# The first modulation of a two-layer trunk in 512 features, summed on TensorE, and its later parts in 1 MB tiles

## The chip, the cores and the metric

One core of a Trainium2 chip runs the whole program. The metric is the device time of one execution in microseconds (us), the median of several runs. The engines are TensorE (PE, with its weight loads as PEld), VectorE (DVE), ScalarE (ACT), GpSimd (POOL) and SyncE (SP), which here does nothing but issue DMA transfers, in order.

## The reference

Two layers work on 256 tokens of 2048 features. A conditioning vector c gives each layer six modulation vectors, and each mixer and each MLP sees a normed input that these scale and shift:

```python
cond = jax.nn.silu(c)
for i in range(DEPTH):
    mod = (cond @ w_mod[i] + b_mod[i])[:, None, :]
    sh_m, sc_m, g_m, sh_f, sc_f, g_f = jnp.split(mod, 6, axis=-1)
    h = rmsnorm(x, norm_mix[i]) * (1.0 + sc_m) + sh_m
    y = gla_mixer(h, ...) if i % 2 == 0 else fox_mixer(h, ...)
    x = x + (1.0 + g_m) * y
    h = rmsnorm(x, norm_ffn[i]) * (1.0 + sc_f) + sh_f
    x = x + (1.0 + g_f) * conv_ffn(h, ...)
return rmsnorm(x, norm_final)
```

Layer 0 is the gated linear attention (GLA). Its first product is `h @ w_in` with 6160 columns: q and k of 1024 each, v and r of 2048 each, and a of 16. Everything is fp32. `w_mod` has 2048 x 12288 numbers per layer, so that one section of it (sc_m, say) is 16.8 MB.

## The kernel before, in words

**The stream.** Nearly all the work is products of the 256 tokens with weights that are read once. A weight tile is 128 rows (one K tile) by 1024 columns, 512 KB. ACT casts it to a high part `wh`, DVE subtracts for a low part `wl` (`split_w`, L112), and TensorE multiplies wh by the high and low part of h and wl by the high part. In `stream_a` (L603) that is 24 matmuls of 256 columns for a K tile, in `stream_b` (L637, for v) 12 of 512. `next_w` (L561) hands out the tiles in the order of the list `plan`; DVE and ACT split up to AHEAD = 3 tiles ahead of TensorE, and SP loads ahead as far as the pool `ring` has free buffers. After each K tile `tick` may run a piece of side work.

**The staging of GLA's input.** h of K tile k needs sc_m and sh_m of 128 features, which are sums over all 2048 rows of `w_mod`. BLOCKS = (8, 8) splits the K tiles in two blocks. Before the stream starts, `drain_startup` makes sc_m and sh_m for the first 8 K tiles (1024 features) out of sixteen 1 MB tiles `wm`: for the first four K rows 8 matvecs each on TensorE (L265, "direct"), for the other twelve one accumulating DVE instruction over 1024 columns each (L271), then 8 transposes (L304), two DVE reductions (L308) and small adds. In between stand the load of x, its transposes (`load_x`, L441), the copies and squares on ACT (L443, L462), the sum over features (L483) and the reciprocal root (`token_rstd`, L492 to L496). Then the pieces q, a, k, v0, v1, r0, r1 run over K tiles 0 to 7 and their sums are put aside in SBUF by `fold` (L707). Meanwhile the tasks for sc_m and sh_m of the features 1024 to 2047 run in the background, in 512 KB tiles of the pool `ring`, on DVE. `drain_bg` ends them, and the same pieces run over K tiles 8 to 15.

**What sets the order.** Each engine runs its instructions in order. The order is that in which the program's scheduler placed them, by a simulated timeline of its own; so instructions that stand later in the code can be placed among earlier ones. A load waits on SP for its buffer to come free and for the load eight places ahead, and every load behind it waits too.

**Pools.** `ring` has 7 buffers of 4 KB per partition (weights, narrow wm tiles), `big` 12 of 8 KB (x, wide wm tiles, h, the put-aside pieces).

Of the kernel before, what the change touches and what calls it, by code (L numbers as in the profile page):

```python
# [18 lines left out]
P = 128  # L19
D = 2048  # L20
# [11 lines left out]
RING = 7  # L32
AHEAD = 3
DIRECT = 4
XAFTER = 1
# [5 lines left out]
PEND = 2  # L41
BLOCKS = (8, 8)
FIRST = (6, 0)
# [27 lines left out]
def kernel(  # L71
# [13 lines left out]
    accp = ctx.enter_context(tc.tile_pool(name="accp", bufs=2))  # L85
    tmp = ctx.enter_context(tc.tile_pool(name="tmp", bufs=2))
# [25 lines left out]
    def split_w(src, moving, after=None):  # L112
        n_ = src.shape[-1]
        o1, o2 = (0, 0) if moving else HELD
        hi = tmp.tile([P, WCOLS], F32R, tag="wh", bufs=AHEAD + 1, name=nm("wh"))[:, o1:o1 + n_]
        lo = tmp.tile([P, WCOLS], F32R, tag="wl", bufs=AHEAD + 1, name=nm("wl"))[:, o2:o2 + n_]
        nc.scalar.copy(out=hi, in_=src)  # L117
        with ExitStack() as es:
            if after is not None:
                es.enter_context(tc.issue_after(after))  # L120
            order["v"] = nc.vector.tensor_tensor(out=lo, in0=src, in1=hi.bitcast(F32), op=ALU.subtract).ins  # L121
# [114 lines left out]
    def mod_tasks(l, key, f0=0, fn=D, wide=False, direct=0, defer=False, turn=False):  # L236
# [8 lines left out]
        def chunk(c0, kt, st):  # L245
            def load():
                st[kt] = bigt([P, per, width], "wm") if wide else ringt([P, per, width], "wm")
                src = w_mod[l, kt * P:(kt + per) * P, s * D + c0:s * D + c0 + width]
                with after_startup(not wide):
                    dma = nc.sync.dma_start(out=st[kt], in_=src.rearrange("(k p) m -> p k m", p=P))  # L250
                if wide:
                    startup["loads"].append(dma.ins)

            def f():
                wt = st.pop(kt)
                m0, mn = c0 // P, width // P
                last = kt + per == KT
                if direct and kt == 0:
                    st["p"] = psA.tile([P, 512], F32, tag="a", name=nm("pd"))
                for j in range(per):  # L260
                    k = kt + j
                    col = cT[:, k:k + 1]
                    if k < direct:
                        for m in range(mn):
                            nc.tensor.matmul(st["p"][:, m:m + 1], wt[:, j, m * P:(m + 1) * P], col,  # L265
                                             start=(k == 0 and m == 0), stop=(k == direct - 1), skip_group_check=True)
                    elif k == direct:
                        st["a"] = accp.tile([P, 1024], F32, tag="acc", name=nm("acc"))[:, :width]
                        nc.vector.tensor_scalar(out=st["a"], in0=wt[:, j, :], scalar1=col, scalar2=None, op0=ALU.mult)
                    else:  # L270
                        nc.vector.scalar_tensor_tensor(out=st["a"], in0=wt[:, j, :], scalar=col, in1=st["a"],  # L271
                                                       op0=ALU.mult, op1=ALU.add)
                if last and defer:
                    deferred.append(finish)
                elif last and wide:
                    finish()
# [11 lines left out]
            def finish():  # L288
# [7 lines left out]
                elif turn or wide:  # L296
                    red = tmp.tile([P, 8], F32, tag="red", name=nm("red"))
                else:
                    pt = misc()
                    nc.tensor.matmul(pt[:, :4 * mn], quad, st["r"][:, :4 * mn], start=True, stop=True)  # L300
                for q0 in range(0, mn if turn or wide else 0, 4):
                    pt = psA.tile([P, 512], F32, tag="a", name=nm("pt")) if wide else misc()
# [13 lines left out]
                if defer or turn or wide:  # L316
# [6 lines left out]
                if direct:  # L323
                    nc.vector.tensor_tensor(out=dst, in0=dst, in1=st["p"][:, :mn], op=ALU.add)
# [107 lines left out]
    def load_x():  # L432
        xs = []
        for tt in range(TT):
            xs.append(bigt([P, D], "xtok"))
            nc.sync.dma_start(out=xs[tt], in_=x[0, tt * P:(tt + 1) * P, :])
        for m in range(0, KT, 2):
# [123 lines left out]
    def next_w(kt, cols, hold=None):  # L561
# [3 lines left out]
        run, look = AHEAD if hold is None else hold, RING - 1  # L565
# [5 lines left out]
    def split_to(end, look=RING - 1):  # L571
# [124 lines left out]
    def gla(l, h):  # L696
# [514 lines left out]
    k0 = 0  # L1211
    for nb in BLOCKS:
        for i, c0 in enumerate((0, 1024, 2048, 3072, 4096, 5120)):
            if i == (0 if k0 + nb == KT else 1):
                plan.append((gla_w_in[0], k0, nb, ((6144, RANK),), False))
            plan_stream(gla_w_in[0], range(k0, k0 + nb), [(c0, 1024)], c0 in (2048, 3072))
        k0 += nb
# [11 lines left out]
    def queue_norm(f0, nb, *kind):  # L1229
        queue(mod_tasks(0, "sc_m", f0 * P, nb * P, *kind, turn=True))  # L1230
        queue(mod_tasks(0, "sh_m", f0 * P, nb * P, *kind, turn=True))

    def drain_startup():
        while bg or pending:
            prefetch(WIDE)
            bg_step()

    queue_norm(0, BLOCKS[0], True, DIRECT)
    for _ in range(XAFTER):
        prefetch(WIDE)  # L1240
        bg_step()
    load_x()
    first_h = make_h(0, "m")
    drain_startup()
    bounds = [sum(BLOCKS[:i]) for i in range(len(BLOCKS))]
# [9 lines left out]
    args = gla(0, h)  # L1255
# [79 lines left out]
```

## Time and profile before

| what | value |
|---|---|
| time, median of 3 runs | 2452.31 us (2449.97 to 2458.36) |
| profiled execution: time, span | 2452.57 us, 2450.8 us |
| PE, PEld busy | 2401.6 us, 2313.5 us |
| DVE, ACT busy | 1926.7 us, 1254.9 us |
| moved by DMA | 638.32 MB, mean 260 GB/s |
| first matmul of the stream | 60.90 us after the span's start |
| end of the 8 tiles of block one of every piece, first matmul of K tile 8 | about 206.2 us |

The profiled execution's time is 1.8 us longer than its span, and its time stands 0.26 us from the median. All times within the program are counted from the span's start. "Granted clock" is the share of TensorE's full clock that the profile shows for a stretch of time.

### The profile page before, as it was taken

How to read it: one execution, taken by the hardware profiler on the slowest of the kernel's cores; microseconds unless marked ns; L12 is line 12 of the kernel's file. 1: busy time of each engine (PE TensorE's matmuls, PEld its weight loads, DVE VectorE, ACT ScalarE, POOL GpSimd, SP SyncE). 2: the span in 40 equal slices, each digit the busy share in tenths (PEclk: the TensorE clock that was granted, in tenths of full speed). 3: DMA queues.
4: the chain of work that ended last, by engine and by line, in shares of the span. 5: the costliest groups of instructions: out<-in, count | busy, mean ns of one | idle time of the engine just before them, and what ended most of it. 6: DMA issues, size and time to landing. Idle time of an engine off the chain costs nothing.

```text
span 2450.8 us, 46953 instructions
## 1 busy us (share of the span) xinstructions
PE 2401.6 (98%) x19147; PEld 2313.5 (94%) x19150; DVE 1926.7 (79%) x2587; ACT 1254.9 (51%) x1700; POOL 16.5 (1%) x35
## 2 busy tenths in 40 slices
PE   6999999999999999999999999999999999999998
PEld 6998899899999999999988888999999999999998
DVE  7777989887789999987587898887876777777544
ACT  2456555444655555543454545554655555555433
POOL 0000000000000000000000000000000000000000
PEclk7999999899999999999999999999999999999999
DMA  9897878798668888999589887687677777756553
GB/s 371 281 314 239 301 260 313 277 315 313 201 192 273 304 290 307 308 336 320 182 287 311 302 291 235 222 292 250 220 236 233 233 235 237 230 194 220 192 190 112
DMA packets 184309, 638.32 MB, mean 260 GB/s; under 512 B 23961, under 2 KB 24971, under 8 KB 183708
## 3 DMA queue, kind: packets, MB, share of 16 engines
q1 hardware_dynamic: 183128, 634.12, 76.8%
q8 instruction: 150, 2.46, 0.4%
q10 hardware_dynamic: 964, 1.20, 0.1%
q14 instruction: 67, 0.55, 0.1%
HBM read 633.14 MB, written 2.10 MB: 259 GB/s over the span
## 4 chain that ended last, share of the span: by engine, by line
PE 88%; DVE 5%; DMA 5%; issue 1%; ACT 0%; SPq 0%; DVEq 0%; ACTq 0%
PE pa L614 23%; PE pa L613 23%; PE pa L612 23%; PE pa L650 5%; PE pa L649 5%; PE pa L648 5%; DMA wm<-in_w_mod_dram 4%; DVE wl L121 2%; DVE acc L271 1%; PE pm L483 0%; PE pt L293 0%; PE pm L852 0%; DMA w<-in_gla_w_in_dram 0%; PE pm L1063 0%; PE pm L874 0%
## 5 line engine op out<-in xcount | busy, mean ns | idle before, releaser
L117 ACT CAST wh<-w 128x1024 fp32r<-128x1024 f32 x819 | 855.9, 1048 | 985.4 <-PE pa L613 686.2
L121 DVE TENSOR_TENSOR wl<-w,wh 128x1024 fp32r<-128x1024 f32 x819 | 993.4, 1219 | 315.5 <-ACT wh L117 311.3
L613 PE MATMUL pa<-h,wh 128*128 128x256 f32 x3584 | 992.3, 278 | 2.3 <-DVE h L530 2.3
L614 PE MATMUL pa<-h,wl 128*128 128x256 f32 x3584 | 990.8, 278 | 3.5 <-DVE wl L121 3.5
L612 PE MATMUL pa<-h,wh 128*128 128x256 f32 x3584 | 990.6, 278 | 3.3 <-ACT h L528 1.8
L614 PEld LDWEIGHTS pa<-h,wl 128*128 128x128 f32 x3584 | 673.1, 188 | 7.1 <-DVE wl L121 4.5
L613 PEld LDWEIGHTS pa<-h,wh 128*128 128x128 f32 x3584 | 675.5, 189 | 3.3 <-DVE h L530 3.1
L612 PEld LDWEIGHTS pa<-h,wh 128*128 128x128 f32 x3584 | 673.6, 189 | 4.4 <-ACT h L528 2.2
L271 DVE SCALAR_TENSOR_TENSOR acc<-wm,cT,acc 128x1024 f32<-128x1024 f32 x352 | 451.9, 1284 | 131.0 <-DMA wm<-in_w_mod_dram 129.4
L613 PE MATMUL pa<-op,wh 128*128 128x256 f32 x1920 | 527.9, 277 | 0.4 <-DVE op L546 0.4
L612 PE MATMUL pa<-op,wh 128*128 128x256 f32 x1920 | 527.2, 277 | 0.0
L614 PE MATMUL pa<-op,wl 128*128 128x256 f32 x1920 | 523.6, 277 | 0.4 <-DVE wl L121 0.4
L613 PEld LDWEIGHTS pa<-op,wh 128*128 128x128 f32 x1920 | 360.5, 188 | 0.6 <-DVE op L546 0.6
L612 PEld LDWEIGHTS pa<-op,wh 128*128 128x128 f32 x1920 | 359.8, 188 | 0.0
L614 PEld LDWEIGHTS pa<-op,wl 128*128 128x128 f32 x1920 | 357.3, 188 | 0.8 <-DVE wl L121 0.6
L649 PE MATMUL pa<-wh,h 128*128 128x512 f32 x512 | 200.1, 392 | 0.0
L648 PE MATMUL pa<-wh,h 128*128 128x512 f32 x512 | 198.7, 392 | 0.0
L650 PE MATMUL pa<-wl,h 128*128 128x512 f32 x512 | 194.3, 393 | 0.0
L1115 ACT ACTIVATE y<-u,cw 128x256 f32<-128x256 f32 x176 | 101.8, 599 | 30.9 <-DVE act L1131 28.6
L648 PEld LDWEIGHTS pa<-wh,h 128*128 128x128 f32 x512 | 96.2, 188 | 19.3 <-issue 0.2
L650 PEld LDWEIGHTS pa<-wl,h 128*128 128x128 f32 x512 | 95.9, 188 | 19.5 <-DVE wl L121 0.3
L649 PEld LDWEIGHTS pa<-wh,h 128*128 128x128 f32 x512 | 96.2, 188 | 19.1
(258 smaller groups left out, 1350.6 us busy)
## 6 DMA issues: line engine op xcount, KB each, us to landing
wm<-in_w_mod_dram SPq DMA_DIRECT2D x352, 512.0 KB, 5.2
w<-in_ffn_w_up_dram SPq DMA_DIRECT2D x320, 512.0 KB, 4.5
w<-in_ffn_w_down_dram SPq DMA_DIRECT2D x176, 512.0 KB, 4.5
w<-in_fox_w_in_dram SPq DMA_DIRECT2D x128, 512.0 KB, 5.0
w<-in_gla_w_in_dram SPq DMA_DIRECT2D x96, 512.0 KB, 5.1
wm<-in_w_mod_dram SPq DMA_DIRECT2D x16, 1024.0 KB, 12.3
w<-in_gla_w_out_dram SPq DMA_DIRECT2D x32, 512.0 KB, 6.0
w<-in_ffn_w_up_dram SPq DMA_DIRECT2D x64, 256.0 KB, 4.1
```

The costliest lines, as they stand in the source:

```text
L117: nc.scalar.copy(out=hi, in_=src)
L121: order["v"] = nc.vector.tensor_tensor(out=lo, in0=src, in1=hi.bitcast(F32), op=ALU.subtract).ins
L271: nc.vector.scalar_tensor_tensor(out=st["a"], in0=wt[:, j, :], scalar=col, in1=st["a"], op0=ALU.mult, op1=ALU.add)
L612: nc.tensor.matmul(o, wh[:, ms], rh, start=(first and m % 2 == 0), stop=False, skip_group_check=True)
L613: nc.tensor.matmul(o, wh[:, ms], rl, start=False, stop=False, skip_group_check=True)
L614: nc.tensor.matmul(o, wl[:, ms], rh, start=False, stop=last, skip_group_check=True)
L648: nc.tensor.matmul(o, lh[:, ts_], wh[:, hs_], start=first, stop=False)
L649: nc.tensor.matmul(o, ll[:, ts_], wh[:, hs_], start=False, stop=False)
L650: nc.tensor.matmul(o, lh[:, ts_], wl[:, hs_], start=False, stop=last)
L1115: nc.scalar.activation(y, u, AF.Identity, scale=cw[:, l * 3 + 2, r:r + 1], bias=cw[:, 6 + l, r:r + 1])
```

## The change

Sections and pools first: `ring` has 8 buffers and the look-ahead of the loads is written out as 6, as it was. Up to three background tiles are loaded ahead (PEND = 3; before 2). The split parts have a pool of their own.

What is computed before the stream starts is sc_m and sh_m of the first 512 features (HEAD = 4 K tiles) out of eight 1 MB tiles of 4 K rows by 512 columns. They are summed on TensorE: `cz` holds silu(c), one column in 32, the rest zero, and for each K row a matmul of 32 result rows by 512 columns is made (`early_sum`); the four K rows of a tile go to the four groups of 32 result partitions of one PSUM bank. ACT copies the bank, and one matvec for each 128 features adds the 128 partitions up and turns the sum (`early_finish`). After three of the four tiles of sh_m five filler matmuls are issued (KEEP). x is loaded after two wm tiles.

The pieces q, k and v0 then run over K tiles 0 to 3. During them sc_m of features 512 to 1023 is summed in the background on DVE (1 MB tiles), and the tiles of sh_m are loaded; at the end `finish_late` sums sh_m on TensorE. Then q, k, v0 run over K tiles 4 to 7 and are added to what was put aside; a, v1, r0, r1 run over K tiles 0 to 7. The features 1024 to 2047 follow in the background in 1 MB tiles of the pool `big` and are ended without `turn`: by DVE transposes and one small matmul with `quad`.

```diff
-RING = 7
+RING = 8
+LOOK = 6
-DIRECT = 4
-XAFTER = 1
-PEND = 2
+PEND = 3
+HEAD = 4
+HEADED = ('q', 'k', 'v0')
+KEEP = 5
...
+    cz = bigt([P, KT, 32], "cz")
+    nc.vector.memset(cz, 0.0)
...
+    nc.vector.tensor_copy(out=cz[:, :, 0:1], in_=cT.rearrange("p (k o) -> p k o", o=1))
...
-        k0 = 0
-        for bi, nb in enumerate(BLOCKS):
-            kts = list(range(k0, k0 + nb))
-            k0 += nb
-            if bi > 0:
-                drain_bg()
-            if bi + 1 < len(BLOCKS):
-                for key, c0 in pieces[1:2] + pieces[:1] + pieces[2:]:
-                    fold(key, piece(key, kts, c0))
+        run(HEADED, ALL[:HEAD])
+        drain_bg()
+        finish_late()
+        run(HEADED, ALL[HEAD:BLOCKS[0]])
+        run([key for key, _ in pieces if key not in HEADED], ALL[:BLOCKS[0]])
+        drain_bg()
+        kts = ALL[BLOCKS[0]:]
...
+    def early_sum(key, f0, j):
+        wt = early.pop((key, f0, j))
+        if j == 0:
+            early[key, f0] = psA.tile([P, 512], F32, tag="a", name=nm("pe"))
+        for g in range(4):
+            mm = nc.tensor.matmul(early[key, f0][32 * g:32 * g + 32, :], cz[:, 4 * j + g, :], wt[:, g, :],
+                                  start=(j == 0), stop=(j == 3), skip_group_check=True)
+        return mm.ins
+
+    def early_finish(key, f0):
+        rows_ = t2("er")
+        nc.scalar.copy(out=rows_, in_=early.pop((key, f0)))
+        pt = misc()
+        for m in range(HEAD):
+            nc.tensor.matmul(pt[:, m:m + 1], rows_[:, m * P:(m + 1) * P], one, start=(m == 0), stop=(m == HEAD - 1),
+                             skip_group_check=True)
+        dst = mod[:, SECT[key], f0:f0 + HEAD]
+        b0 = SECT[key] * KT + f0
+        nc.vector.tensor_tensor(out=dst, in0=pt[:, :HEAD], in1=bm[:, b0:b0 + HEAD], op=ALU.add)
...
+    todo = [(key, 0, j) for key in ("sc_m", "sh_m") for j in range(4)]
+    for args in todo[:2]:
+        startup["loads"].append(early_load(*args))
+    xs = fetch_x()
+    for args in todo[2:WIDE]:
+        startup["loads"].append(early_load(*args))
+    load_x(xs)
     first_h = make_h(0, "m")
-    drain_startup()
+    for i, args in enumerate(todo):
+        if i + WIDE < len(todo):
+            startup["loads"].append(early_load(*todo[i + WIDE]))
+        summed = early_sum(*args)
+        if args[2] == 3:
+            early_finish(*args[:2])
+        elif args[0] == "sh_m":
+            pw = psA.tile([P, 512], F32, tag="a", name=nm("pw"))
+            with tc.issue_after(summed):
+                for _ in range(KEEP):
+                    nc.tensor.matmul(pw, fill[:, :P], fill, start=True, stop=True)
...
     def staged_h(m):
-        i = bounds.index(m) if m in bounds else KT
-        if i + 1 < len(BLOCKS):
-            queue_norm(bounds[i + 1], BLOCKS[i + 1])
-            set_pace(6 * BLOCKS[i] - N0)
+        if m == 0:
+            for j, task in enumerate(mod_tasks(0, "sc_m", HEAD * P, HEAD * P, wide=True)):
+                bg.extend((task, (lambda j=j: early_load("sh_m", HEAD, j), lambda: None)))
+            set_pace(HEAD * len(HEADED) - 3)
+        elif m == HEAD:
+            for key in ("sc_m", "sh_m"):
+                queue(mod_tasks(0, key, BLOCKS[0] * P, BLOCKS[1] * P, wide=True))
+            set_pace(6 * BLOCKS[0] - HEAD * len(HEADED) - N0)
         return first_h(m)
```

How the scheduler places this, at three places. In the order lists below, a row is a line of the kernel, an operation, the tiles written and read, and a size; x4 stands for four alike.

TensorE, the start, before (pd: direct matvecs, pm<-ident,xtok: transposes of x) and then with the change (pe: early sums, pw: fillers):

```order
L173 MATMUL pm_110<-ident,crow_101 128x16
L265 MATMUL pd_147<-cT,wm_139 128x1 x16
L265 MATMUL pd_147<-cT,wm_141 128x1 x16
L177 MATMUL pm_114<-ident,rows_103 128x98
L197 MATMUL pm_131<-ident,brow_129 128x96
L197 MATMUL pm_136<-ident,brow_134 128x96
L441 MATMUL pm_168<-ident,xtok_164 128x128
```

```order
L1246 MATMUL pe_239<-wm_153,cz_123 32x512 x3
L1246 MATMUL pe_239<-wm_155,cz_123 32x512 x4
L203 MATMUL pm_137<-ident,brow_135 128x96
L1246 MATMUL pe_271<-wm_237,cz_123 32x512 x4
L1283 LDWEIGHTS fill
L1283 MATMUL pw_276<-fill 128x512
...
L203 MATMUL pm_142<-ident,brow_140 128x96
L431 MATMUL pm_157<-ident,xtok_149 128x128
L431 MATMUL pm_157<-ident,xtok_150 128x128
```

The first transposes of x stood right after the small transposes; now they stand behind the fifth early sum (wm_237, the first tile of sh_m) and its fillers. The other 28 stand behind the sixth, seventh and eighth sum.

SP, the loads that follow the eight early tiles, with the change (w: weight tiles; of the wm tiles L256 loads sc_m, L1239 sh_m, features 512 to 1023):

```order
L571 DMA w_454<-in_gla_w_in_dram 128x1024
L256 DMA wm_382<-in_w_mod_dram 128x4x512
L1239 DMA wm_384<-in_w_mod_dram 128x4x512
L256 DMA wm_386<-in_w_mod_dram 128x4x512
L1239 DMA wm_446<-in_w_mod_dram 128x4x512
L256 DMA wm_500<-in_w_mod_dram 128x4x512
L571 DMA w_456<-in_gla_w_in_dram 128x1024
...
L571 DMA w_547<-in_gla_w_in_dram 128x1024
L1239 DMA wm_545<-in_w_mod_dram 128x4x512
L256 DMA wm_577<-in_w_mod_dram 128x4x512
L1239 DMA wm_613<-in_w_mod_dram 128x4x512
```

Five of the eight tiles are issued after the eighth weight tile (w_454), the last three after the fourteenth (w_547). Before, nothing of this kind stood here: the stream's first block had its modulation whole.

TensorE and then DVE, the passage from K tile 3 to K tile 4, with the change (pa_661: the last bank of v0; h_775: h of K tiles 4 to 7; wl_794: the low part of q's weight tile for K tile 7; pm_698 and pm_765: the finished sums of sc_m and sh_m):

```order
L640 MATMUL pa_661<-wl_665,h_318 128x512
L1246 MATMUL pe_746<-wm_384,cz_123 32x512 x4
L1246 MATMUL pe_746<-wm_446,cz_123 32x512 x4
L1246 MATMUL pe_746<-wm_545,cz_123 32x512 x4
L1246 MATMUL pe_746<-wm_613,cz_123 32x512 x4
L295 MATMUL pm_698<-red_649,quad 128x16
L1255 MATMUL pm_765<-ones,er_763 128x1 x4
L602 MATMUL pa_771<-h_775,wh_682 128x256
```

```order
L124 TENSOR_TENSOR wl_726<-w_583,wh_725 128x1024
L279 TENSOR_REDUCE red_649<-mt_650 128x16
L124 TENSOR_TENSOR wl_794<-w_615,wh_793 128x1024
L311 TENSOR_TENSOR mod<-pm_698,bm 32x4 x4
L315 SCALAR_TENSOR_TENSOR mod<-mod,vec 128x4
L1259 TENSOR_TENSOR mod<-pm_765,bm 128x4
L519 TENSOR_SCALAR hn_776<-hn_776,mod 128x256
```

The sums of sh_m stand between the last matmul of v0 over K tile 3 and the first of q over K tile 4, and on DVE a weight tile's low part stands ahead of the modulation that K tile 4 waits for. Before, K tile 4 followed K tile 3 with nothing between.

More of the change, by code (lines that the diff above doesn't have):

```diff
@@ L248, in load @@
                 src = w_mod[l, kt * P:(kt + per) * P, s * D + c0:s * D + c0 + width]
[L249 to L252, printed above, removed]
+                with after_startup():
+                    nc.sync.dma_start(out=st[kt], in_=src.rearrange("(k p) m -> p k m", p=P))
             def f():
                 wt = st.pop(kt)
-                m0, mn = c0 // P, width // P
                 last = kt + per == KT
-                if direct and kt == 0:
-                    st["p"] = psA.tile([P, 512], F32, tag="a", name=nm("pd"))
                 for j in range(per):
@@ L262, in f @@
                     col = cT[:, k:k + 1]
[L263 to L267, printed above, removed]
+                    if k == 0:
                         st["a"] = accp.tile([P, 1024], F32, tag="acc", name=nm("acc"))[:, :width]
@@ L295, in finish @@
                     red = pt
-                elif turn or wide:
+                elif turn:
                     red = tmp.tile([P, 8], F32, tag="red", name=nm("red"))
@@ L300, in finish @@
                     nc.tensor.matmul(pt[:, :4 * mn], quad, st["r"][:, :4 * mn], start=True, stop=True)
-                for q0 in range(0, mn if turn or wide else 0, 4):
-                    pt = psA.tile([P, 512], F32, tag="a", name=nm("pt")) if wide else misc()
+                for q0 in range(0, mn if turn else 0, 4):
+                    pt = misc()
                     for m in range(min(4, mn - q0)):
@@ L430, with fetch_x, load_x @@
     xT = const.tile([P, KT, T], F32, name="xT")
-    def load_x():
-        xs = []
+    def fetch_x():
+        xs = [bigt([P, D], "xtok") for _ in range(TT)]
         for tt in range(TT):
-            xs.append(bigt([P, D], "xtok"))
             nc.sync.dma_start(out=xs[tt], in_=x[0, tt * P:(tt + 1) * P, :])
+        return xs
+    def load_x(xs):
         for m in range(0, KT, 2):
@@ L564, in next_w @@
         fetched["use"] += 1
-        run, look = AHEAD if hold is None else hold, RING - 1
+        run, look = AHEAD if hold is None else hold, LOOK
         if i < STAGE:
@@ L569, in next_w, with split_to @@
         return splits.popleft()
-    def split_to(end, look=RING - 1):
+    def split_to(end, look=LOOK):
         while fetched["split"] < end:
@@ L1209, in queue_halves, with plan_piece @@
                 queue(mod_tasks(l, key + kind, f0, 1024, defer=f0 > 0 and DEFER))
[L1211 to L1217, printed above, removed]
+    gla_cols = {"q": 0, "k": 1024, "v0": 2048, "v1": 3072, "r0": 4096, "r1": 5120}
+    def plan_piece(key, kts):
+        if key == "a":
+            plan.append((gla_w_in[0], kts[0], len(kts), ((6144, RANK),), False))
+        else:
+            plan_stream(gla_w_in[0], kts, [(gla_cols[key], 1024)], key[0] == "v")
+    for key in HEADED:
+        plan_piece(key, ALL[:HEAD])
+    for key in HEADED:
+        plan_piece(key, ALL[HEAD:BLOCKS[0]])
+    for key in ("a", *gla_cols):
+        if key not in HEADED:
+            plan_piece(key, ALL[:BLOCKS[0]])
+    for key in ("a", *gla_cols):
+        plan_piece(key, ALL[BLOCKS[0]:])
     for g in range(2):
@@ L1228 @@
     load_bmod()
[L1229 to L1242, printed above, removed]
-    first_h = make_h(0, "m")
-    drain_startup()
-    bounds = [sum(BLOCKS[:i]) for i in range(len(BLOCKS))]
@@ new lines, with finish_late @@
+    bounds = [0, HEAD, BLOCKS[0]]
+    def finish_late():
+        for j in range(4):
+            early_sum("sh_m", HEAD, j)
+        early_finish("sh_m", HEAD)
+    def staged_h(m):
+        if m == 0:
[6 more added lines that the diff above has]
+            set_pace(6 * BLOCKS[0] - HEAD * len(HEADED) - N0)
```

37 lines of the change are left out of this document (22 added, 15 removed).

## The prediction

> **What bounds the kernel now.** I read the page first, then TensorE's waits, then tables by stretch of time.
>
> ```profile
> span 2450.8 us, 46953 instructions
> PE 2401.6 (98%) x19147; PEld 2313.5 (94%) x19150; DVE 1926.7 (79%) x2587; ACT 1254.9 (51%) x1700; POOL 16.5 (1%) x35
> PEclk7999999899999999999999999999999999999999
> ```
>
> TensorE is busy for 98% of the span. So a change of this size can gain only where TensorE waits, runs at a low clock, or does work that isn't the product. The clock's low digits are in the first slice, and a little in slice 8. TensorE's waits, all of the time from 206 us on, the three largest:
>
> ```profile
> PE pm L300 <- DVE red L284: 4.0, 4, 1.8
> PE pm L483 <- DVE ss L476: 3.9, 1, 3.9
> PE pa L614 <- DVE wl L121: 2.6, 4, 0.9
> ```
>
> Some 11 us in 2245, so what follows block one is as good as full. The time to be won lies ahead of 206 us. Stretches (us; busy PE, PEld, DVE, ACT, POOL with counts; granted clock; DMA share, GB/s):
>
> ```profile
> 40.00:60.00 20.00, 13.41 (x60) 12.75 (x60) 17.51 (x21) 2.56 (x3) 0.00 (x0) 0.50 0.95 378
> 60.90:64.30 3.40, 2.17 (x9) 1.88 (x9) 3.37 (x8) 3.40 (x6) 0.00 (x0) 0.50 0.00 0
> 64.30:69.90 5.60, 5.60 (x26) 5.60 (x27) 5.60 (x10) 2.06 (x3) 0.00 (x0) 0.51 0.76 201
> 69.90:101.30 31.40, 31.40 (x278) 31.40 (x277) 23.95 (x33) 14.17 (x17) 0.00 (x0) 1.00 0.90 299
> 195.11:198.18 3.07, 0.28 (x4) 0.08 (x2) 1.34 (x2) 1.04 (x1) 0.00 (x0) 1.00 0.84 332
> 198.18:206.20 8.02, 8.02 (x56) 8.02 (x57) 4.26 (x7) 5.07 (x21) 0.00 (x0) 0.79 0.67 209
> ```
>
> A warm stream makes 278 matmuls in 31.40 us: 0.113 us each, 2.71 us for a K tile of 24. The first 9.0 us (60.9 to 69.9) make only 35 of them, at half clock. Ahead of the stream stand 60.9 us, and at the end of block one 3.07 us of waiting and a dip of the clock. What ends last before the stream:
>
> ```profile
> 49.18 7.88 DVE L271 SCALAR_TENSOR_TENSOR acc<-wm,cT,acc 128x1024 f32<-128x1024 f32 x6
> 57.12 1.97 PE L304 MATMUL pt<-ident,acc 128*128 128x128 f32 x8 [5.67 <-DVE acc L271]
> 60.25 1.09 ACT L528 ACTIVATE h<-hn,mod 128x256 fp32r<-128x256 f32 x2 [4.87 <-DVE mod L324]
> 60.90 1.22 PE L612 MATMUL pa<-h,wh 128*128 128x256 f32 x4 [1.82 <-ACT h L528]
> ```
>
> So the order is: the sixteenth wm tile, DVE's sums, transposes, h.
>
> **The change part by part.**
>
> *The start.* Half the wm bytes and all of DVE's sums go. Bytes moved from 0 to 29.0 us and from 0 to 49.2 us, and three stretches:
>
> ```profile
> DMA packets 2885, 10.68 MB, mean 368 GB/s; under 512 B 266, under 2 KB 572, under 8 KB 2629
> DMA packets 5047, 18.93 MB, mean 385 GB/s; under 512 B 419, under 2 KB 725, under 8 KB 4789
> 5.00:30.00 25.00, 21.55 (x99) 19.55 (x99) 13.30 (x18) 7.69 (x14) 0.00 (x0) 1.00 1.03 410
> 915.00:945.00 30.00, 30.00 (x265) 29.94 (x264) 28.02 (x35) 17.60 (x28) 0.00 (x0) 1.00 0.95 327
> 70.00:180.00 110.00, 110.00 (x779) 102.41 (x778) 80.81 (x82) 54.71 (x78) 0.00 (x0) 1.00 0.92 309
> ```
>
> Eight wm tiles, x and the small rows are 10.7 MB: there at 29 us, instead of 18.9 MB at 49. The new tiles have rows of 2 KB. From 915 to 945 us ffn_w_up is loaded largely in such rows, 327 GB/s at a share of 0.95; 4 KB rows give 309 at 0.92. No loss, so I add none.
>
> Then the early sums. Prices of a 512-column fp32 matmul, and of matmuls in different result partitions:
>
> ```profile
> 223.78 1.98 PE L751 MATMUL pm<-wg,aT 17*128 17x512 f32 x4
> L751 PE MATMUL pm<-wg,aT x8: 587/588/692, 223.8 to 230.5; 17*128 17x512 f32 x8
> 290.49 0.22 PE L852 MATMUL pm<-q,k 128*64 128x64 f32 x1
> 290.49 0.22 PE L852 MATMUL pm<-q,kend 128*64 128x64 f32 x1
> 290.99 0.50 PE L650 MATMUL pa<-wl,h 128*128 128x512 f32 x1
> 198.18 1.09 PE L304 MATMUL pm<-ident,acc 128*128 128x128 f32 x8 [2.79 <-DVE acc L271]
> ```
>
> Four of 512 columns take 1.98 us, with the last one's 0.59 us tail: 0.46 us apart at full clock, and 0.93 at half (the 8 transposes: 1.09 us warm, 1.97 at half clock). Attention scores go to partitions 0 to 63 or 64 to 127, and two of them start within the same 0.01 us. So a tile's four column groups cost between 0.46 us (side by side) and 1.84 (in turn), twice that at half clock. I take side by side, because those two rows are the only ones with groups. The Trainium skill speaks to both ends ("TensorE: Matmul & The Clock Gate", Part 3): it has three column tiles at 2.38 times one, and four row tiles at 3.07 times; my estimate from it is 1.84 / 3.07 = 0.60 us for a tile, which would move the sum by less than 1 us. The switch between full and grouped use costs about 0.1 us in the last L852 row and the L650 row after it (0.16 us between last start and next, of which one such matmul is 0.06); some 14 switches lie in the start, where TensorE waits for tiles anyway. The skill's page "TensorEngine Tiling (Array Packing)", Key Properties, says that a change of tiling mode drains TensorE, without a price; by the row it is 1.4 us, hidden.
>
> So sums keep up with the tiles (one each 1.05 MB / 410 GB/s = 2.6 us), and x's chain ends last. ACT's part of it before:
>
> ```profile
> 22.58 0.58 ACT L443 COPY xT<-pm 128x512 f32<-128x512 f32 x1 [16.23 <-PE pm L441]
> 31.03 1.19 ACT L462 ACTIVATE sq<-xT 128x512 f32<-128x512 f32 x2
> 32.23 1.28 ACT L492 ACT_TABLE_LOAD   x1
> 42.73 0.47 ACT L492 ACTIVATE rb<-pm,epsc 128x256 f32<-128x256 f32 x1 [9.22 <-PE pm L483]
> 47.84 1.42 DVE L527 TENSOR_TENSOR hn<-xT,rb 128x256 f32<-128x256 f32 x4
> ```
>
> The first transposes now stand behind the fifth sum: three tiles ahead of the last, 29 - 7.7 = 21.3 us, plus the sum 0.9, five fillers at half clock 2.2 (a 512-column pass of the warm stream takes 2.71 / 12 = 0.226 us, twice that is 0.45), four transposes 1.0: 25.4. ACT's copies and squares took 9.65 us (22.58 to 32.23). They now also wait between batches for the sixth to eighth sum, for which I add 2: 37. Then two copies of sums (1.2), the table load (1.3), rb (0.5), three DVE steps of 0.42 and two of 0.17 (1.6), four hn (1.4), the last add and h (0.8), hand-overs of some 0.03 to 0.1 each (1): 44.8, say 45 us. That is **-15.9 us**, between -19 (no waits in ACT) and +1 (the first rival). The first 9.0 us of the stream are as cold as they were, since TensorE has little to do from 33 to 45 us: 0.
>
> *K tile 3 to 4.* New, and on the path: TensorE has nothing else, as the order shows. Sixteen sum matmuls: 4 x 0.46 = 1.9 us (7.4 in turn). Then ACT's copy 0.58, four matvecs about 0.7 with their tail, the add 0.2, h 0.6, hand-overs 0.4: 4.4 us together. DVE's wl_794 waits for v0's last weights and costs a cast and 1.2 us, ending ahead of that. After the 3.07 us wait at 195 us the clock was 0.79 for 8.02 us, 1.7 us lost; I add it. **+6 us**, between +3 and +11.
>
> *K tile 7 to 8.* Wait (2.8) and dip (1.7) are 4.5 us now, because the last wm tile landed late. It is now issued about eight weight tiles earlier in the queue. In its place comes a chain of the quad matmul, four small adds and h, 1.5 us. **-3 us**, between -4.5 and +2.
>
> *DVE in K tiles 4 to 7.* The put-aside pieces cost adds there which they did not before:
>
> ```profile
> L121 DVE TENSOR_TENSOR wl<-w,wh 128x1024 fp32r<-128x1024 f32 x49 | 58.8, 1218 | 0.6 <-ACT wh L117 0.6
> L271 DVE SCALAR_TENSOR_TENSOR acc<-wm,cT,acc 128x1024 f32<-128x1024 f32 x30 | 38.5, 1283 | 34.6 <-DMA wm<-in_w_mod_dram 34.6
> L725 DVE TENSOR_TENSOR q<-q,pa 128x512 f32<-128x512 f32 x4 | 2.6, 680 | 0.0
> ```
>
> Twelve low parts (14.6 us), twelve adds (8.2) and the eleven sums placed among them (14.1) are 36.9 us of DVE in 12 x 2.71 = 32.5 us of TensorE. DVE is up to three tiles (8.1 us) ahead, which covers the 4.4 us. **+1**, between 0 and +5.
>
> *Later.* A third tile on its way (PEND, ring of 8) acts on the 6.6 us that TensorE waits for L284 and L121 in the list above, where DVE is held up by late wm tiles. **-1.5**, between -6 and 0.
>
> Sum: -15.9 + 6 - 3 + 1 - 1.5 = -13.4. The profiled execution took 2452.57 us (span and 1.8 us around it; the median is 2452.31), so **2439 us**.
>
> **The rivals.**
>
> *The groups take turns, and the start stays at half clock* (slower). For it: the clock was 0.50 from 40 to 60 us although TensorE counted as busy for 13.41 of 20. Eight sums of 3.7 us, 15 fillers of 0.45, 32 transposes of 0.25 are 44 us from 7 us on; then 10.5 us from the last transposes to h: the stream starts at 61.5. With 7.4 us of sums at K tile 4 the passage costs 11.5: +0.6 + 11.5 - 3 + 1 - 1.5 = +8.6, 2461 us. It decides once a tile's sum takes more than the 2.6 us of its load. Against it are the two rows at 290.49. The same Part 3 of "TensorE: Matmul & The Clock Gate" says that a weight load overlaps running matmuls only where the row group differs, and the four groups here share all rows: by that rule this rival holds.
>
> *Modulation for K tile 4 comes late* (same). v0 over K tile 3 ends at 45 + 9 + (12 x 2.71 - 35 x 0.113) = 82.6 us. From 29 us on, 14 weight tiles and eight wm tiles must land, 15.7 MB: 67 us at 410 GB/s, 80 at 309, 108 at the 201 that the stretch from 64.3 shows, where SP waited for buffers. Here only the last six weight tiles wait for DVE, so I expect about 70. Were it 94, all but 2 us would be gone: 2450.
>
> *DVE binds in K tiles 4 to 7* (same): h of four K tiles uses up its lead right after the passage, and then the 4.4 us and one K tile's delay (2.7) show: +7, 2446.
>
> *The start does not shrink as it says* (same): x's chain runs behind cold sums and fillers and the stream starts at 52: 2446.
>
> **How the numbers follow.** About 0.3%, 7.4 us, is what a measurement can tell from no change. Forecast 0.64 (its own range 2431 to 2445, all faster), late modulation 0.10, DVE 0.07, late start 0.08 (all three within 0.3%: 0.25), groups in turn 0.11 (slower). The range takes in all but the last and the far ends: 2430 to 2456.
>
> **What would show it.** The first L602 matmul at about 45 us; each tile's four L1246 matmuls starting within 0.05 us of each other; L1246 of wm_256 done by 33. A gap of about 4 to 5 us, sums included, at K tile 4 near 83 to 88 us, with wm_613 landed by 75. K tile 8 reached at about 194 us. From there to the end as before, some 2245 us. Wrong: a start after 55 us, sums of over 2 us for a tile, a wait for wm tiles at K tile 4, or waits for wl from 95 to 125 us.

## Result, and the profile after

| | before | after |
|---|---|---|
| median of 4 runs each, us | 2452.86 (2449.97 to 2458.36) | 2429.93 (2429.0 to 2430.48) |
| ratio, 95% interval | | 0.9904 (0.9886 to 0.9921) |
| profiled execution: time, span, us | 2452.57, 2450.8 | 2429.0, 2427.0 |

The change is faster, by 22.9 us; 2439 had been predicted, with 2430 to 2456 as the range, and the median lies just below its end. So the direction was right, and the gain is 1.7 times the forecast 13.4 us. One of the six executions of e3_full_width_sums, an experiment below, took 6695 us against 2443 to 2447 of the others, and is left out of its figures. The page after:

```profile
span 2427.0 us, 46850 instructions
PE 2384.6 (98%) x19127; PEld 2285.0 (94%) x19131; DVE 1922.6 (79%) x2609; ACT 1252.4 (52%) x1671; POOL 16.2 (1%) x35
PEclk9999999999999999999999999999999999999999
```

The clock's low first digit is gone, though the start is still partly cold, as the rows below show. To see where the gain arose, I cut both profiled executions at the same places of the program: the first matmul of the stream, the first matmul of K tile 8, the norm ahead of layer 0's MLP, and the norm ahead of layer 1's mixer. Lengths in us, read from the starts of the matmuls there:

| stretch | before | after | difference |
|---|---|---|---|
| to the stream | 60.90 | 43.66 | -17.2 |
| stream to K tile 8 | 145.3 | 148.8 | +3.4 |
| K tile 8 to the norm ahead of the MLP | 260.7 | 262.2 | +1.6 |
| from there to the norm ahead of layer 1's mixer | 745.8 | 733.3 | -12.5 |
| from there to the end | 1238.1 | 1239.0 | +0.9 |
| span | 2450.8 | 2427.0 | -23.8 |

**The start.** TensorE's timeline after (start, duration, both in us; a row joins neighbours of one kind):

```profile
7.33 1.93 PE L1246 MATMUL pe<-wm,cz 128*32 128x512 f32 x8 [4.49 <-DVE cz L190]
32.37 1.06 PE L1246 MATMUL pe<-wm,cz 128*32 128x512 f32 x8
33.37 1.09 PE L431 MATMUL pm<-ident,xtok 128*128 128x128 f32 x8
34.70 0.66 PE L431 MATMUL pm<-ident,xtok 128*128 128x128 f32 x4 [0.24 <-ACT xT L433]
38.64 0.67 PE L473 MATMUL pm<-ss,onesD 128*128 128x256 f32 x2 [3.29 <-DVE ss L466]
43.66 1.22 PE L602 MATMUL pa<-h,wh 128*128 128x256 f32 x4 [1.22 <-ACT h L518]
47.02 0.58 PE L604 MATMUL pa<-h,wl 128*128 128x256 f32 x1 [1.23 <-DVE wl L124]
```

The last early sum stands at 32.37 us and the chain of x follows it: transposes to 35.4, the sum over features at 38.64, the stream at 43.66. A tile of four sum matmuls has eight records (x8), and the next matmul starts 1.00 us after the first of them at full clock. The tile at 7.33 us took 1.93 us for its eight records, so that the first sums ran at about half clock; the page's digit does not show it, because the trace has no clock on record before 23.1 us and counts that time as full.

**K tiles 4 and 8.** The same timeline at the two passages:

```profile
80.58 3.64 PE L1246 MATMUL pe<-wm,cz 128*32 128x512 f32 x32
84.16 0.40 PE L295 MATMUL pm<-red,quad 128*128 128x16 f32 x2
84.93 1.05 PE L1255 MATMUL pm<-ones,er 128*128 128x1 f32 x8 [0.38 <-ACT er L1252]
86.87 0.74 PE L602 MATMUL pa<-h,wh 128*128 128x256 f32 x4 [0.89 <-ACT h L518]
190.25 0.30 PE L295 MATMUL pm<-red,quad 128*128 128x32 f32 x2
192.41 0.38 PE L652 MATMUL pm<-h,wh 128*128 128x256 f32 x1 [1.86 <-ACT h L518]
```

Between 80.58 and 86.87 the stream stands for 6.3 us, and at 190.25 for 2.2. Each is followed by half clock. Stretches after (columns as in the prediction: length, busy times with counts, granted clock, DMA):

```profile
43.66:47.02 3.36, 2.13 (x9) 1.84 (x9) 3.33 (x8) 3.31 (x5) 0.00 (x0) 0.50 1.05 386
47.02:50.40 3.38, 3.38 (x16) 3.38 (x17) 3.38 (x5) 0.00 (x0) 0.00 (x0) 0.50 1.05 387
87.90:91.40 3.50, 3.50 (x17) 3.50 (x18) 3.14 (x10) 0.39 (x1) 0.00 (x0) 0.51 1.01 412
192.40:200.00 7.60, 7.13 (x45) 6.93 (x46) 7.26 (x22) 4.89 (x8) 0.00 (x0) 0.78 0.37 128
```

**From 455 us on.** Here lies the surprise, 12.5 us. The stretch itself, before and after:

```profile
466.89:1212.67 745.78, 737.81 (x6406) 732.47 (x6407) 620.82 (x787) 387.44 (x489) 0.00 (x0) 0.99 0.81 277
```

```profile
454.66:1187.96 733.30, 731.03 (x6405) 728.92 (x6407) 621.43 (x787) 388.39 (x490) 0.00 (x0) 1.00 0.83 283
```

The same work (6406 and 6405 matmul records, 787 DVE instructions), 12.5 us shorter. And DVE's accumulation of the background modulation in the same stretch, before and after; the last figures of a row are DVE's idle time just ahead of these instructions and what ended most of it:

```profile
L271 DVE SCALAR_TENSOR_TENSOR acc<-wm,cT,acc 128x1024 f32<-128x1024 f32 x120 | 153.9, 1282 | 58.8 <-DMA wm<-in_w_mod_dram 57.9
```

```profile
L268 DVE SCALAR_TENSOR_TENSOR acc<-wm,cT,acc 128x1024 f32<-128x1024 f32 x120 | 153.2, 1278 | 0.1
```

In this stretch DVE waited 57.9 us for late wm tiles, and now hardly at all. Over the whole execution the same row of the page has 129.4 us before and 0.3 after. Of the 129.4, 24.4 us lie behind the stretch, where the change gains nothing (+0.9 in the table): a wait of DVE is not yet a loss of TensorE. The reason for the late tiles is the short lead. In the stretch a wm tile lands 5.3 us (median) after its issue before the change, and 5.4 after it; DVE starts on it 6.0 us (median) after its issue before, and 10.0 after, with issues and uses paired in their order. In the page's chain of waits, by line, the same showed; before and after:

```profile
PE pa L614 23%; PE pa L613 23%; PE pa L612 23%; PE pa L650 5%; PE pa L649 5%; PE pa L648 5%; DMA wm<-in_w_mod_dram 4%; DVE wl L121 2%; DVE acc L271 1%; PE pm L483 0%; PE pt L293 0%; PE pm L852 0%; DMA w<-in_gla_w_in_dram 0%; PE pm L1063 0%; PE pm L874 0%
```

```profile
PE pa L604 25%; PE pa L603 25%; PE pa L602 25%; PE pa L640 5%; PE pa L639 5%; PE pa L638 5%; DMA wm<-in_w_mod_dram 1%; DVE wl L124 1%; PE pe L1246 0%; PE pm L473 0%; DVE acc L268 0%; PE pm L846 0%; PE pm L868 0%; PE pm L1057 0%; PE pt L288 0%
```

These are shares of the whole span. In the stretch alone the chain has 8.3% of wm before, some 62 us, and next to nothing after.

### The profile page after: what moved, and what is told of

Same layout as the page of the kernel before. It is cut to its first block, busy times and chain, and to the rows that moved or that the text cites. A ratio compares the mean times of both kernels' runs of the same rounds, so it can differ in the third digit from the quotient of the medians.

```text
span 2427.0 us, 46850 instructions
## 1 busy us (share of the span) xinstructions
PE 2384.6 (98%) x19127; PEld 2285.0 (94%) x19131; DVE 1922.6 (79%) x2609; ACT 1252.4 (52%) x1671; POOL 16.2 (1%) x35
## 4 chain that ended last, share of the span: by engine, by line
PE 95%; DVE 3%; DMA 1%; ACT 1%; issue 1%; DVEq 0%; SPq 0%
PE pa L604 25%; PE pa L603 25%; PE pa L602 25%; PE pa L640 5%; PE pa L639 5%; PE pa L638 5%; DMA wm<-in_w_mod_dram 1%; DVE wl L124 1%; PE pe L1246 0%; PE pm L473 0%; DVE acc L268 0%; PE pm L846 0%; PE pm L868 0%; PE pm L1057 0%; PE pt L288 0%
## 5 line engine op out<-in xcount | busy, mean ns | idle before, releaser
L602 PE MATMUL pa<-h,wh 128*128 128x256 f32 x3584 | 987.7, 278 | 2.1 <-ACT h L518 2.1
L602 PEld LDWEIGHTS pa<-h,wh 128*128 128x128 f32 x3584 | 672.3, 188 | 4.9 <-ACT h L518 2.3
L602 PE MATMUL pa<-op,wh 128*128 128x256 f32 x1920 | 526.3, 277 | 0.0
L268 DVE SCALAR_TENSOR_TENSOR acc<-wm,cT,acc 128x1024 f32<-128x1024 f32 (+1 forms) x345 | 433.2, 1256 | 1.0 <-DMA wm<-in_w_mod_dram 0.3
L602 PEld LDWEIGHTS pa<-op,wh 128*128 128x128 f32 x1920 | 360.2, 188 | 0.0
```

The costliest lines, as they stand in the source:

```text
L602: nc.tensor.matmul(o, wh[:, ms], rh, start=(first and m % 2 == 0), stop=False, skip_group_check=True)
```

## Experiments

The runs come from several rounds. Their times can be set side by side: the last stretch of the table, from the norm ahead of layer 1's mixer to the end, takes 1238.1 to 1240.2 us in all fourteen profiled executions. A ratio is always to the kernel before in the same round, and that kernel's median moved from 2452.6 to 2457.4 us between rounds (single executions from 2447.2 to 2463.6), so that small differences between ratios of different rounds say little.

Theory after the result: the third tile on its way (PEND = 3) gives the 12.5 us, and the new staging the rest. The rival: the staging does it all, since its background work stands otherwise. Other runs ask which part of the staging carries its gain, and what its passages cost.

### The third tile apart from the staging

The changed kernel with two tiles:

```diff
-RING = 8
+RING = 7
-PEND = 3
+PEND = 2
```

> The changed kernel with two background tiles ahead and a ring of 7, as before the change; all else as changed. Theory: some 10 of the 23 us gained come from the third tile on its way, which lets the modulation tiles of 512 KB land before VectorE needs them. Then this kernel takes 2438 to 2442 us, VectorE waits for wm for over 60 us again, and TensorE's losses between 460 and 980 us come back; the stream still starts at 43 to 44 us. Rival: the later waits vanished because the stream stands better after the new start, or because of the 1 MB tiles; then 2429 to 2432 us and few waits.

Measured: 2444.27 us, ratio to before 0.9949 (0.9931 to 0.9968). The kernel before with three tiles:

```diff
-RING = 7
+RING = 8
-PEND = 2
+PEND = 3
-        run, look = AHEAD if hold is None else hold, RING - 1
+        run, look = AHEAD if hold is None else hold, RING - 2
...
-    def split_to(end, look=RING - 1):
+    def split_to(end, look=RING - 2):
```

> The kernel before with three background tiles ahead and a ring of 8, the look-ahead kept at 6; the start and the staging are as before. Theory of the third tile: 2440 to 2444 us, the first matmul of the stream still at about 61 us, VectorE's 129 us of waiting for wm mostly gone. Rival (the new start or the 1 MB tiles did it): 2450 to 2454 us.

Measured: 2432.94 us, ratio 0.9896 (0.987 to 0.9922). So two constants in the old kernel bring it within 3.0 us of the whole change; by the ratios the two cannot be told apart. The theory's direction holds, but its size was still too small. The same stretch and DVE's row in it, first with the staging alone, then with the third tile alone:

```profile
458.05:1205.68 747.63, 734.63 (x6405) 729.86 (x6407) 620.80 (x787) 387.09 (x489) 0.00 (x0) 1.00 0.81 277
L268 DVE SCALAR_TENSOR_TENSOR acc<-wm,cT,acc 128x1024 f32<-128x1024 f32 x120 | 153.8, 1282 | 65.7 <-DMA wm<-in_w_mod_dram 65.3
```

```profile
460.44:1194.83 734.39, 731.89 (x6405) 729.86 (x6407) 621.80 (x787) 388.32 (x490) 0.00 (x0) 1.00 0.82 282
L271 DVE SCALAR_TENSOR_TENSOR acc<-wm,cT,acc 128x1024 f32<-128x1024 f32 x120 | 153.4, 1279 | 0.4 <-DMA wm<-in_w_mod_dram 0.3
```

With two tiles the stretch takes 746 to 748 us and DVE waits 58 to 65 us in it for wm; with three it takes 733 to 734 and DVE waits 0.3 us or less, whatever the staging. The lead from issue to use is 6.0 us (median) with two tiles and 10.0 with three, in either staging. In the old staging the third tile does one thing more: from the stream to K tile 8 that kernel takes 139.7 us instead of 145.3, because the 3.07 us of waiting at K tile 8 and its half clock are gone. This is why the gains of the two parts do not add: on top of the third tile the staging takes 17.4 us from the start and gives back 9.1 us ahead of K tile 8 (148.8 against 139.7) and 2.6 us behind it.

### Is it the buffer or the tile on its way?

The changed kernel with three tiles ahead, but the old number of buffers:

```diff
-RING = 8
+RING = 7
```

> The changed kernel with a ring of 7 buffers in place of 8, three background tiles ahead as changed. If the earlier issue of the modulation tiles alone is what removes the waits: 2429 to 2433 us. If the third tile only helps because it has a buffer of its own, and otherwise takes one from the weight tiles, then weights come late instead: 2436 to 2444 us, as with two tiles ahead (2444 us).

Measured: 2431.06 us, ratio 0.9905 (0.9888 to 0.9921), the same as the change. DVE's wait for wm at L268 is 6.6 us in the whole execution, against 91.0 with two tiles (e1_two_tiles); its lead is 8.0 us. So it is the third tile loaded ahead; the 1.1 us to the change lie within the spread of the four executions (2428.9 to 2433.1).

### The groups one after another

`cz` gets 128 columns instead of 32, so that the four K rows of a tile are summed one after another into all 128 result partitions. The sums are the same.

```diff
-    cz = bigt([P, KT, 32], "cz")
+    cz = bigt([P, KT, P], "cz")
...
-            mm = nc.tensor.matmul(early[key, f0][32 * g:32 * g + 32, :], cz[:, 4 * j + g, :], wt[:, g, :],
-                                  start=(j == 0), stop=(j == 3), skip_group_check=True)
+            mm = nc.tensor.matmul(early[key, f0], cz[:, 4 * j + g, :], wt[:, g, :],
+                                  start=(j == 0 and g == 0), stop=(j == 3 and g == 3), skip_group_check=True)
```

> The changed kernel with the silu(c) columns widened from 32 to 128 columns, so that the four K rows of a tile are summed one after another over all 128 result partitions. Theory: side by side, the four groups hide most of each other; a 512-column fp32 matmul is two recorded passes of 0.43 to 0.46 us, so that a tile takes 3.4 to 3.7 us here at full clock against 1.0 us, and the sums at K tile 4 take 14 us against 3.6. The stream starts 3 to 8 us later and the whole takes 2443 to 2451 us. Rival: groups share the array's inputs and gain nothing that matters; then a tile takes 1.0 us here too and the time is 2429 to 2432 us.

Measured: 2444.61 us, ratio 0.9952 (0.9935 to 0.9969), as expected. The stream starts at 55.97 us, 12.3 later than in the change, where 3 to 8 had been expected. Its timeline:

```profile
24.88 3.62 PE L1246 MATMUL pe<-wm,cz 128*128 128x512 f32 x8
29.94 3.60 PE L1246 MATMUL pe<-wm,cz 128*128 128x512 f32 x8
```

Eight records take 3.6 us instead of 1.06. The four column groups do run side by side in the change, and without that it would have lost 14.7 of its 22.9 us.

### The fillers left out

```diff
-KEEP = 5
+KEEP = 0
```

> The changed kernel without the fifteen filler matmuls between the early sums. Theory A: they cost nothing and hold nothing, since TensorE's clock falls before the stream begins in any case; x's transposes move up by 1 us: 2428 to 2431 us. Theory B: they keep the clock full during the last sums and transposes of x; without them these run at half clock, the stream starts 2 to 3 us later and the whole takes 2432 to 2434 us.

Measured: 2427.61 us, ratio 0.9879 (0.9858 to 0.99). The fillers do not pay where they stand: without them the stream starts at 42.03 us (43.66 with them), and both kernels begin it at half clock. The earlier start is lost again by K tile 8, which comes at 193.2 us (192.4 with the fillers): TensorE waits 4.0 us there for the background sums and h, instead of 1.9. The 2.3 us that the time gains arise behind it.

### The later modulation in narrow tiles

Features 1024 to 2047 in 512 KB tiles of `ring`, ended with `turn`, as before:

```diff
-                queue(mod_tasks(0, key, BLOCKS[0] * P, BLOCKS[1] * P, wide=True))
+                queue(mod_tasks(0, key, BLOCKS[0] * P, BLOCKS[1] * P, turn=True))
```

> The changed kernel with the modulation of features 1024 to 2047 in 512 KB tiles of the ring, ended by transposes on TensorE as before the change. If the 1 MB tiles matter: the passage to K tile 8 waits for late tiles again, 3 to 6 us there, 2433 to 2436 us. If three narrow tiles ahead are enough (as the kernel before with three tiles ahead suggests, whose block one took 139.7 us): 2427 to 2431 us, with a gap of under 1 us at K tile 8 in place of 2.1 us.

Measured: 2428.06 us, ratio 0.9895 (0.988 to 0.991). TensorE's wait at K tile 8 is 3.0 us, where under 1 had been expected with narrow tiles, and yet the time is not above the change's. So the 1 MB tiles for these features, a part that stands in the change's name, bring nothing that the whole time shows; the third tile, which brings most, does not stand in it.

### The sums at K tile 4 behind v1

v1 also runs over K tiles 0 to 3 first, and the sums of sh_m and the first h are issued ahead of it, so that the chain to h lies beside v1's matmuls:

```diff
-HEADED = ('q', 'k', 'v0')
+HEADED = ('q', 'k', 'v0', 'v1')
...
-        run(HEADED, ALL[:HEAD])
+        run(HEADED[:-1], ALL[:HEAD])
...
+        h(HEAD)
+        run(HEADED[-1:], ALL[:HEAD])
```

(The two paces of the background work are counted for the three pieces ahead of the sums, as in the change.)

> The changed kernel with v1 as a fourth piece over K tiles 0 to 3, and sh_m's sums and h of K tile 4 placed ahead of it, so that v1 covers the chain from the sums to h. The passage costs 8.0 us in the changed kernel: 3.6 of sums, some 2.4 of waiting for the chain, and about 1.7 of the low clock that follows. Theory: waiting and dip go, the sums stay: 2425 to 2427 us. Rival: the added put-aside of v1 (four more adds on VectorE) and the later sums of the features from 1024 on cost as much: 2429 to 2432 us.

Measured: 2427.35 us, ratio 0.9892 (0.9878 to 0.9907). At K tile 4 there is no wait and no half clock any more, and yet the stream takes 148.8 us to K tile 8, as in the change. Most of what the passage saved came back: 1.3 us more in the first K tiles (5.4 us lost against 4.1, counted from start to start of the matmuls), and 2.4 us of short stalls between 140 and 155 us, where DVE has no free time:

```profile
140.00:150.00 10.00, 9.12 (x70) 8.28 (x69) 10.00 (x12) 3.53 (x4) 0.00 (x0) 1.00 1.03 410
```

### Fillers just ahead of the stream, and the later sums earlier

Twelve fillers go behind the last transposes of x and ten behind the last early matvecs, none among the sums; and the background sums for features 1024 to 2047 are spread over 27 weight tiles instead of 32, so that they end earlier (the pace has one step for each weight tile; an expectation below calls these half tiles):

```diff
-KEEP = 5
+KEEP = 0
...
+    keep_warm(12, warm["x"].ins)
+    keep_warm(10, warm["m"].ins)
...
-            set_pace(6 * BLOCKS[0] - HEAD * len(HEADED) - N0)
+            set_pace(6 * BLOCKS[0] - HEAD * len(HEADED) - 9)
```

> The changed kernel with its fillers moved: none between the early sums, twelve after the last transpose of x and ten after the last early matvec; and the sums of the features from 1024 on paced to end five K tiles earlier. Theory: the stream starts at about 42 us and at full clock, instead of running 6.8 us at half clock (3.4 us), and the gap at K tile 8 (2.1 us and the dip after it, 1.7) goes: 2422 to 2426 us. Rival: the fillers stand in the way of the sum over x's features and of the matvecs, or the clock falls all the same: 2427 to 2431 us, with the gain at K tile 8 alone.

Measured: 2417.51 us, ratio 0.9855 (0.9841 to 0.987): the fastest of all, 12.4 us ahead of the change. Its timeline ahead of the stream, and a stretch that begins just behind it:

```profile
33.15 2.54 PE L426 MATMUL pw<-fill 128*128 128x512 bf16 x11
38.85 3.93 PE L426 MATMUL pw<-fill 128*128 128x512 bf16 x10
42.43 0.82 PE L611 MATMUL pa<-h,wh 128*128 128x256 f32 x4
```

```profile
43.00:55.00 12.00, 12.00 (x108) 12.00 (x107) 11.73 (x19) 4.57 (x7) 0.00 (x0) 1.00 1.05 388
```

The same stretch of the change:

```profile
43.00:55.00 12.00, 10.11 (x64) 9.82 (x65) 11.32 (x20) 6.07 (x8) 0.00 (x0) 0.69 1.05 388
```

The stream runs at full clock from its first microsecond: 108 matmuls in these 12 us, where the change has 64 at a clock of 0.69. At K tile 8 it does not wait at all. Against the change it is 1.2 us ahead at the start, 5.8 at K tile 8 and 11.5 at the norm ahead of the MLP. Of the 5.7 us between these two, some 2 are the half clock and small waits that no longer follow K tile 8, and 1.6 a shorter wait of TensorE at the norm (2.3 us against 3.9). The two edits apart:

> The changed kernel with only the fillers moved to just before the stream, the pace of the later sums as in the change. Theory: moving the fillers keeps the clock full through the first K tiles (about 4.5 us between the first matmul of the stream and K tile 8, and 1.2 us before it), so 2429 - 5 to -7 = 2422 to 2424 us; the gap of 2.1 us before K tile 8 and its half-clock stretch of 1.7 us stay. Rival: the fillers only postpone the stream and the pace carries the whole gain: 2428 to 2430 us.

> The changed kernel with only the later background sums issued earlier (the divisor of their pace 5 half tiles smaller). Theory: the sums end before K tile 8, the gap of 2.1 us there goes and with it 1.7 us of half clock, and about 1.5 us at the norm before the MLP: 2429 - 4 to -6 = 2423 to 2425 us. Rival: earlier sums only crowd DVE in K tiles 4 to 7 and what K tile 8 gains is lost there: 2427 to 2430 us.

The fillers alone took 2426.43 us (ratio 0.9875, 0.9857 to 0.9894), less of a gain than expected; the pace alone 2423.45 (0.9865, 0.9845 to 0.9884), about as expected. With the fillers alone the early microseconds are won as expected, but TensorE then waits longer at K tile 8:

```profile
PE pm L661 <- ACT h L527: 2.1, 1, 2.1
PE pa L611 <- ACT h L527: 2.0, 1, 2.0
PE pm L295 <- DVE red L279: 1.9, 1, 1.9
```

The first and third row are K tile 8 (4.0 us; the change waited 1.9 there), the second is K tile 4. A stream that comes earlier meets sums that do not; e4_no_fillers, with its earlier start, shows the same 4.0 us there. Of the 3.5 us that the fillers alone gained, 2.3 had come with leaving out the old ones. With the pace they gain 5.9 us (2423.45 to 2417.51). This fits both together giving 12.4 us and each alone 3.5 and 6.5, though the executions of the pace alone spread from 2421.3 to 2426.1.

### Both improvements together

e8's edits and e7's in one kernel:

> The moved fillers and the earlier pace of the run before it, together with v1 as a fourth piece over K tiles 0 to 3 that covers the chain after sh_m's sums. If the two gains are of different places, they add: in the run with moved fillers the passage to K tile 4 still shows 2.9 us of waiting and a dip of 3.4 us at half clock (1.7 us), so 2412 to 2415 us, a ratio of 0.983 to 0.985 to the kernel before. If not, the stream catches up with loads or VectorE in between: 2416 to 2420 us.

Measured: 2425.59 us, ratio 0.9869 (0.9844 to 0.9894). A miss: 8 us slower than without v1 among the first pieces. Its waits from 130 to 200 us:

```profile
PE pm L295 <- DVE red L279: 3.8, 1, 3.8
PE pa L613 <- DVE wl L124: 2.2, 1, 2.2
PE pm L661 <- ACT h L527: 1.4, 1, 1.4
```

I took this for a pace too slow by now and spread the sums over 22 weight tiles instead of 27:

> The kernel e9_both (fillers before the stream, sums of sh_m behind v1) with the later sums issued earlier still (divisor 14 smaller in place of 9). Theory: e9_both lost its gain because at 183.9 us TensorE waited 3.8 us for the reduction of the last background sum on DVE and 1.4 us more for h, with a stretch of half clock: with the sums earlier the wait at K tile 8 goes, 2425.6 - 5 to -8 = 2417 to 2421 us. Rival: with v1 in the first four K tiles DVE has no room for the sums wherever they stand, and the wait moves forward into the stream: 2424 to 2427 us.

Measured: 2427.01 us, ratio 0.9877 (0.9855 to 0.9899), and the same three waits of 3.8, 2.2 and 1.4 us. The theory of the pace falls. The last background sum on DVE starts at 171.0 us in e8_warm_start, at 180.0 in e9_both and at 181.5 here, so a faster pace no longer moves it. Between 97 and 183 us, e8_warm_start first and then e9_both:

```profile
97.00:183.00 86.00, 86.00 (x610) 79.80 (x609) 83.17 (x88) 34.59 (x39) 0.23 (x2) 1.00 0.91 332
```

```profile
97.00:183.00 86.00, 83.82 (x641) 79.86 (x640) 84.03 (x92) 32.89 (x36) 0.00 (x0) 1.00 0.93 345
L724 DVE TENSOR_TENSOR v<-v,pa 128x512 f32<-128x512 f32 x8 | 5.2, 681 | 1.5 <-PE pa L649 1.5
```

DVE is busy for 96.7 and 97.7% of that time, and the fourth put-aside piece brings it four more adds (8 of 0.68 us instead of 4) and a wait of 1.5 us for TensorE. So DVE, full, fits what is seen; that it alone makes the 8 us was not tried.

## Why the prediction was right and wrong

**The step that failed** is the term *Later*: "-1.5, between -6 and 0". Measured from K tile 8 on it is about -11.6 us: -12.5, +0.9 and +1.6 in the table, less the 1.6 us of half clock that now falls behind K tile 8 and belongs to the passage. e1_two_tiles and e2_before_three_tiles show its cause, the third tile. The mechanism was named rightly (DVE held up by late wm tiles), but the size was mis-read in two ways, and what follows block one was not "as good as full".

First, I bounded it by the 6.6 us that TensorE's listed waits for L284 and L121 make, and left the two small rows out. The list counts a wait from the recorded end of the matmul before. But a stream matmul is recorded for 0.28 us and the next starts 0.11 us after it, so that each stall is listed some 0.17 us too short, and short ones not at all. A stall of before, on TensorE and then on DVE:

```profile
585.31 0.28 PE L613 MATMUL pa<-h,wh 128*128 128x256 f32 x1
586.49 0.39 PE L614 MATMUL pa<-h,wl 128*128 128x256 f32 x1 [0.90 <-DVE wl L121]
```

```profile
584.02 1.28 DVE L271 SCALAR_TENSOR_TENSOR acc<-wm,cT,acc 128x1024 f32<-128x1024 f32 x1 [2.31 <-DMA wm<-in_w_mod_dram]
585.22 2.35 DVE L121 TENSOR_TENSOR wl<-w,wh 128x1024 fp32r<-128x1024 f32 x2
```

From start to start 1.18 us pass where 0.11 is the rule: 1.07 lost, 0.90 listed. Its cause stands in DVE's row: 2.31 us for a wm tile, and the low part that TensorE needs is queued behind it. Added up from start to start over the stretch, against the median interval of each kind of matmul, TensorE lost 18.5 us before and 6.5 after, 12.0 apart, which is nearly the whole measured gain of 12.5. Of these, 1.5 lie in the first 28 us, where the norm's own chain ran longer at half clock before, and 10.4 behind it, where the list has 7.5 us of waits before and 0.2 after.

Second, I took 1.5 of the 6.6 without a reason from a row, while the page's row of DVE showed 129.4 us of waiting for wm, and the page's chain gave that load 4% (some 100 us, of which some 20 lie ahead of the stream and 62 in this stretch) and L121 2%. Most of that wait is covered by DVE's lead, which is why 58 us of DVE's time in the stretch bring only some 10 of TensorE's; but it said that this term was the one most in need of a wide bound. By size the second slip is the larger: it leaves out 5.1 us, the list's shortness 3.8.

**The other terms** make -11.9 in the prediction and -12.0 in the profile, with errors that cancel, which is luck:

| term | predicted | measured | |
|---|---|---|---|
| start of the stream | -15.9 | -17.2 | first L602 at 43.66 us instead of 45 |
| cold first K tiles | 0 | -1.0 | 5.1 us lost before, 4.1 now, start to start |
| K tile 3 to 4 | +6 | +8.4 | 6.3 us of passage and 2.2 of half clock and small waits |
| K tile 7 to 8 | -3 | -2.2 | the 16 transposes went; wait and half clock are 4.5 us, as before |
| DVE in K tiles 4 to 7 | +1 | 0 | 0.2 us lost from 95 to 190 us |

At K tile 4 the sums took 3.6 us where 1.9 had been reckoned. A 512-column fp32 matmul appears as two records (the 48 such matmuls of L1246 are 96 records; an fp32 transpose has one, 32 for the 32 of x), and I had taken the "x4 in 1.98 us" of L751 for four matmuls: they are two, so one costs about 0.9 us and not 0.46. Both ends of the price were thus half of what they should have been. That four groups share the time (1.0 us for a tile, against 3.6 one after another) was right. The wait at K tile 8 was expected to be a chain of 1.5 us; it took 2.2, and the half clock came with it.

**The rivals.** The groups taking turns is refuted: 1.06 us for x8 in the change and 3.6 where they are made to. Nor did the start stay at half clock: the granted clock was full from 23.1 to 40.1 us. With the right price of a matmul this rival lay just where e3_full_width_sums measured it: 3.6 us for a tile are more than the 2.6 us of its load. The rule of "TensorE: Matmul & The Clock Gate", Part 3, in the Trainium skill, that a weight load overlaps running matmuls only where the row group differs, does not agree with this case: the four groups share all rows, the loads of all four start within 0.02 us (from 80.58 us on, beside the matmuls that run there), and the groups overlap 3.5 times. The same part of the Trainium skill has 3.07 for four row tiles, which would give 3.6 / 3.07 = 1.17 us, an estimate; 1.00 was measured. Late modulation at K tile 4 did not occur: no wait for a wm tile stands there. DVE did not bind in K tiles 4 to 7, though e9_both and e12_both_earlier show that little is missing. The start shrank as it says.

**Of the signs to look for**, those on the start and on K tile 8 (192.4 us, 194 said) came; the gap at K tile 4 came with 6.3 us, where 4 to 5 had been said; "from there to the end as before, some 2245 us" did not: it is 2234.6 after, and 2244.6 before.

## What to carry to other kernels

Where an engine that feeds TensorE waits for loads, read that engine's own idle time and the chain, and count TensorE's loss from start to start of its matmuls against their steady interval; its listed idle is only a lower bound. But not every such wait costs: of DVE's waits for wm, those in one stretch cost TensorE some 10 us and those behind it nothing. Then try the cheap constant first: one more tile loaded ahead did nearly as much in the old kernel as the whole change did. And when a stream starts earlier or warmer, move the work that it will wait for next by as much, or the gain turns into that wait.

## What the hardware showed that I had not expected

- An fp32 matmul with 512 columns is recorded as two records of 0.45 us, each of them twice the 0.226 us of a 512-column matmul of the stream. One tile of four took 3.6 us one after another (0.9 us each), and 1.0 us in four groups of 32 result columns, with the same rows.
- After TensorE had stood idle for most of 2 to 3 us (84.2 to 86.9 and 190.5 to 192.4), it was granted half clock for some 3.4 us, and this began only 1 to 1.4 us after it had taken up its work: the clock was 0.51 from 87.9 to 91.4, and 0.78 over 192.4 to 200.0. This does not follow every such wait: after one of 1.97 us (469.7 to 471.7) the clock stayed at 1.00, and in e1_two_tiles after one of 3.34 us (534.5 to 537.8) too. With 22 filler matmuls right ahead of the stream, its first 12 us ran at 1.00.
